# Attention issued at a planner offset of 700 in a two-layer hybrid attention backbone

## Chip, cores and metric

One core of a Trainium2 chip runs the whole program. The metric is device time in microseconds (us) of one execution. The engines are TensorE (PE; its weight loads are listed apart as PEld), VectorE (DVE), ScalarE (ACT), GpSimd (POOL) and SyncE (SP). Each works through its own list of instructions in the order fixed when the program is built. An instruction that waits holds up all that stand behind it on its engine. SP issues most DMAs, ACT some.

## What is computed

Two layers over 512 latent tokens and 256 context tokens of width 1024, in float32. Each layer has one mixer with three head groups of eight heads and a gate:

```
def layer(x, cx, ...):
    hx = rmsnorm(x, norm_w) * (1 + scale) + shift          # the context likewise: hc
    px, pc = split_cols(hx @ w_in), split_cols(hc @ w_in)  # q, k, v of A, B, C, and the gate
    ya, yca = global_gqa(...)            # A: all latent and all context keys; RMS-normed q/k, rotary
    yb, ycb = neighbourhood_attn(...)    # B: a window of 8 x 16 on the grid, learned bias, plus context
    yc_, ycc = window_gqa(...)           # C: +-128 tokens, a sink logit per head, plus context
    ux = concatenate([ya, yb, yc_]) * silu(px[9])
    x = x + gate * (ux @ w_out)          # the context likewise, except in the last layer
```

The result is the latent stream after a final RMS norm.

## The kernel before

**Numbers.** Every float32 operand of a product is split into a rounded high part (fp32r) and a low remainder, and a product is three matmuls (high x high, high x low, low x high). For weights, `split` (L244) copies a staged tile `ws` to `wh` on ACT (L247) and subtracts on DVE or POOL to get `wl` (L250). Three staging buffers and five pairs of split buffers run ahead of the matmuls.

**Projections.** `proj_f` (matmuls at L318, up to 512 columns) and `proj_t` (L341, 256 columns, two token tiles to a bank) multiply the normed stream `hL`, `hC` by the weights into a PSUM bank `pj`, of which there are two. When a bank is complete, a function `done` handles the result: for A's q and k it copies the bank to `qs` (L821), squares, applies norm and rotary (L830 to L840, on POOL for most q), splits into `qd`, transposes `qd` on PE into a bank T (L899) and copies T to `qt` on ACT (L902). For C it copies to `tA` (L973); after it, DMAs swap halves into `tB`, POOL multiplies and adds (L979 to L981), and Q and K are split on ACT and POOL (L989, L990). For gates it takes a tanh `th` (L879) and a multiply (L880).

**Attention.** A pair of heads is one entry of work, with one unit per head (two per head for A) and, in the first layer, one more per head for the context queries. A unit's `scores` multiply Q by K into the PSUM tensor `Sbig` (matmuls at L1049), take the negated maximum `negm` on DVE (L1158, L1121, or with a mask or bias added L1208 and L1265) and the exponential `P` on ACT (L1160, L1127, L1211, L1267). Its `values` transpose P into a bank T (L1054; two banks, shared with `done`), copy it to `pth` on ACT (L798), subtract on DVE to `ptl` (L1044), and multiply both by V into `Obig` (L1049). `finish` (L1315) divides by the sums, applies the gate and stores the pair's result `u`. B's bias is built inside `scores` when first needed: two loads on SP, a row `wr` (L1437) and a mask `bm` (L1440), and three additions on POOL (L1445). In `attend` (L1375) a unit's values run with the next unit's scores, so a pair's last values and its `finish` fall into the next stage.

**Stages.** The list `PLAN` (L33) sets the order: first projections alone; then, stage by stage, the attention of one pair is woven with the projections that later pairs need: B0 to B3, then A0, C0, A1, C1, A2, C2, A3. Last comes C3, woven with the first columns of the output projection (`head`, matmuls at L519). So the q of A1 is projected while C0 attends, and the q of C1 while A1 attends.

**Order.** `weave` (L1407) takes steps of attention and of projection in turn, in proportion to estimates in the planner's own units (`TA`, L1503, and `time`, L1520; they follow the columns streamed at full rate): in the second layer 16.5 for an A pair, 12.5 for a B or C pair, 10.6 for one pair's q and gate. It also ties every third projection matmul behind an attention matmul that stands `lead` = 6 of these units earlier in the same stage (`paced`, L296), so that projections do not run further ahead than that.

The framework's planner turns this into the lists. Each instruction takes the next number of a counter. The planner simulates the engines, and an engine that is free takes, among the instructions whose inputs and buffers are ready, the one with the lowest number. A block under `high_priority(offset=n)` numbers its instructions from n below the counter, and hands the counter back as it was. All `done` calls stand in such blocks, with offset 600 (`hp`, `hpf`). Weight loads and splits, the projections' matmuls and the attention take the counter as it is. Only the last attention (`rest`, C3) stands in blocks already, of offset 0 (`hr`).

Of the kernel before, what the change touches and what calls it, by code (L numbers as in the profile page):

```python
# [19 lines left out]
D = 1024  # L20
# [26 lines left out]
AT_ONCE = (2, 3)  # L47
RSPAN = 7 * 31 + 48

CFG = dict(lead=6.0, hp=600, hpf=600, pj=2, T=2, O=1, P=5, qt=5, kt=4, vt=4, gt=3, wh=5, ws=3, pt=3, bm=2, tA=1, OT=1, u=1, tl=1, ab="pj", tR=1, map={}, ada=2, h0=300, h1=1000, a0=9, H=2, hr=0, cp="A", cv="A", w0="D", w1="D", w2=(("D", "D"), ("D", "D")), hb="D", ws_="P")  # L50

WT_A_KV, WT_A, WT_BV, WT_BG = 0, 1, 5, 7
WF_BQ, WF_BK, WF_CQ, WF_CK, WF_CV, WF_CG = 0, 4, 8, 12, 13, 14
# [10 lines left out]
def body(tc, xT, small, bcast, rpb, adaw, adat, wt, wf, wo, trigA, trigC, mskB, mskC, outT):  # L64
    nc = tc.nc
    es = ExitStack()
    const = es.enter_context(tc.tile_pool(name="const", bufs=1))
    wpool = es.enter_context(tc.tile_pool(name="w", bufs=CFG["wh"]))
    hpool = es.enter_context(tc.tile_pool(name="h", bufs=16))
# [21 lines left out]
    def pj():  # L91
        return ps.tile([128, 512], F32, name="pj", bufs=CFG["pj"])

    Sbig = ps.tile([128, 1536], F32)

    def psT():
        return ps.tile([128, 512], F32, name="T", bufs=CFG["T"])

# [57 lines left out]
    class Dots:  # L156


        def __init__(self):
            self.jobs = [(h, j) for h in range(2) for j in range(KT)]  # L160
            self.n = self.at = self.wait = 0
            self.room = [qkv.tile([128, 3, 512], F32, name="dots", tag="vt", bufs=CFG["vt"]) for _ in range(2)]
            self.rows(0)
# [77 lines left out]
    pace = {"at": None, "pe": None, "dve": None, "sp": None}  # L241
    wlo = {"n": 0, "by": CFG["w0"]}

# [10 lines left out]
    def load_w1(dram_ap, i, shape):  # L254
        st = wpool.tile([128, 512], F32, name="ws", bufs=CFG["ws"])
        pace["sp"] = nc.sync.dma_start(st, dram_ap[:, i * 512:(i + 1) * 512]).ins.name
        return split(st, shape)
# [284 lines left out]
    for l in range(2):  # L542
        last = l == 1
        with tc.tile_pool(name=f"p1_{l}", bufs=1, reuse_waits="tile") as p1:
            mixers(tc, nc, l, last, p1, ps, const, dict(locals()))
# [226 lines left out]
def mixers(tc, nc, l, last, p1, ps, const, env):  # L772
    g_ = env
# [179 lines left out]
    def tables_c():  # L953
        for c in range(2):
            t = p1.tile([128, NT], F32, name=f"tabx{c}", tag=f"tab{c}", bufs=1)
            nc.sync.dma_start(t, trigC[c])
            tabs["C", c] = t
# [330 lines left out]
    def units(kind, i, Q, K, V, G, extra):  # L1288
        c = dict(kind=kind, i=i, Q=Q, G=G)
        out = []  # L1290
        for h in range(2):
            if kind == "B":
                vh, k, sink = h, K[h], None
                box = []

                def bm(h=h, box=box):
                    if not box:
                        box.append(extra(2 * i + h))
                    return box[0]
            else:  # L1300
                vh = i // 2
                k = K[vh]
                j = l * 8 + 2 * i + h
                sink = negsink[:, j:j + 1] if kind == "C" else None
                bm = (lambda: extra)
            v = lambda kb, vh=vh: V[:, kb, vh].rearrange("p x f -> p (x f)")
            if kind == "A":
                out += [GlobalUnit(c, h, k, v, tiles=t) for t in ((0, 1), (2, 3))]
            else:
                out.append((NearUnit if kind == "B" else BandUnit)(c, h, k, v, sink, bm))  # L1310
            if not last:
                out.append(CtxUnit(c, h, k, v, sink))
        return c, out
# [57 lines left out]
    def chain(gens):  # L1371
        for g in gens:
            yield from g

    def attend(pair):  # L1375

        if pair is not None:
            c, us = pair
            for n, un in enumerate(us):
                sc = un.scores()  # L1380
                yield from zipped(chain(pend), sc)
                pend.clear()
                pend.append(un.values())
            pend.append(finish(c, c["kind"] == "C" and c["i"] == 3))

    def zipped(a, b):

        ta = tb = 0.0
        a, b = iter(a), iter(b)
        la = lb = True  # L1390
        while la or lb:
            if la and (ta <= tb or not lb):
                try:
                    x = next(a)
                    ta += x
                    yield x
                except StopIteration:
                    la = False
            else:
                try:  # L1400
                    x = next(b)
                    tb += x
                    yield x
                except StopIteration:
                    lb = False

    def weave(a, ta, b, tb, lead=CFG["lead"]):  # L1407

        xa = xb = 0.0
        la = a is not None  # L1410
        past = []
        pace["pe"] = None
        while True:
            if la and xa * tb <= xb * ta:
                try:
                    xa += next(a)
                    past.append((xa, pace["pe"]))
                except StopIteration:
                    la = False
            else:  # L1420
                while len(past) > 1 and past[1][0] <= xa - lead:
                    past.pop(0)
                pace["at"] = past[0][1] if past and past[0][0] <= xa - lead else None
                try:
                    xb += next(b)
                except StopIteration as r:
                    pace["at"] = None
                    if la:
                        for _ in a:
                            pass  # L1430
                    return r.value
# [24 lines left out]
    def bias_c():  # L1456
        m = p1.tile([128, 896], F32, name="msk", tag="bm", bufs=CFG["bm"])
        nc.sync.dma_start(m, mskC)

        def bm(i):  # L1460
            return m[:, (384, 256, 0, 0)[i]:(896, 896, 640, 512)[i]]
        return bm
# [5 lines left out]
    def ada_pre():  # L1468
        if ada_jobs:
            job = ada_jobs.pop(0)  # L1470
            ada_next.append((job, ada_load(job, g_["qkv"], "vt", CFG["vt"])))
# [13 lines left out]
    def with_ada(gen, t, k):  # L1485

        n, x, nxt = 0, 0.0, t / 2 / max(k, 1)
        while True:
            try:
                y = next(gen)  # L1490
            except StopIteration as r:
                while n < k:
                    one_piece()
                    n += 1
                return r.value
            x += y
            if x > nxt and n < k:
                one_piece()
                n += 1
                nxt += t / k  # L1500
            yield y

    TA = {"A": 16.5, "B": 12.5, "C": 12.5, None: 1.0}  # L1503
    TC = 0.0 if last else 2.7
    tq = 5.3 if last else 7.8
    prev = None
# [17 lines left out]
    def work(items, bank):  # L1524
        for k, i in items:
            made[k, i] = yield from make[k](i, bank)
# [4 lines left out]
    for pair, items, n_ada in PLAN:  # L1531
        if pair is None and not last:

            items = items[1:] + items[:1]
        if pair is not None:
            kind, i = pair
            if kind == "B":
                Q, K = made["b", i]
                prev = units("B", i, Q, K, made["v", i // 2][i % 2], lambda i=i: made["g", i // 2][i % 2], bmb)
            else:  # L1540
                Q, G = made[kind.lower(), i]
                K, V = made[kind.lower() + "kv", 0]
                prev = units(kind, i, Q, K, V, G, bmc if kind == "C" else None)
        if pair == ("A", 0):
            tables_c()
            bmc = bias_c()
            if not last:
                ada_pre()
        wlo["by"] = CFG["w1"] if pair is None or pair[0] == "B" else CFG["ws_"]
        t = sum(time[k] for k, i in items)  # L1550
        gen = with_ada(work(items, first if pair is None else pj), t, n_ada[last])

        soon = 1.5 if last and pair == ("A", 3) else 1.0
        weave(attend(prev) if prev else None, TA[kind] + TC if prev else 1.0, gen, t * soon)
    Q, G = made["c", 3]
    K, V = made["ckv", 0]
    prev = units("C", 3, Q, K, V, G, bmc)

    def rest():
        yield from attend(prev)  # L1560
        yield from chain(pend)

    def urgent(gen):
        while True:
            with tc.high_priority(offset=CFG["hr"]):
                try:
                    x = next(gen)
                except StopIteration:
                    return
            yield x  # L1570

    weave(urgent(rest()), TA["C"] + TC, g_["head"](l, p1), CFG["H"] * (7.5 if last else 8.0), 3.0)


def col_index():
# [95 lines left out]
```

## Time and profile before

| what | value |
|---|---|
| time, median of 3 runs | 1198.84 us (1198.54 to 1199.2) |
| span of the profiled execution, from its first to its last instruction (the profile gives no other time of it) | 1197.7 us |
| PE busy | 1150.5 us, 8016 matmuls |
| DVE, ACT, POOL busy | 769.4, 696.9, 408.1 us |
| mean granted PE clock | 0.996 of full |
| scores of B, first and second layer (from L1265) | 86 to 257 us, 738 to 886 us |
| scores of A, first and last in a layer (L1158) | 268 to 550 us, 888 to 1103 us |
| scores of C, first and last in a layer (L1208) | 325 to 580 us, 930 to 1129 us |
| bytes moved by DMA | 124.22 MB |

"Busy" of PE counts each matmul from its start to its modelled end, which overlaps the next one, so a PE that is busy all the time need not be at its peak. An idle stretch of PE is one in which no matmul was under way at all. Below, lines of a list read: start, duration, engine, line of the kernel, operation, result <- operands, shape, count, and in brackets the engine's idle time just before and what ended it. A line with "<-" and a colon reads: who waited, for whom, in total us, how often, the longest.

### The profile page before, as it was taken

The numbers are of one execution on the slowest core, as the hardware profiler recorded it, in microseconds if no ns is written. First come the engines' busy times: TensorE is split into PE (matmuls) and PEld (weight loads), VectorE is DVE, ScalarE is ACT, GpSimd is POOL, SyncE is SP. The second block draws the span as 40 slices with busy tenths as digits, with TensorE's granted clock in tenths as the row PEclk, the third lists the DMA queues.
The fourth block names the chain that finished last, engine by engine and source line by source line (L and its number), as shares of the span: only waits on it lengthen the run. The fifth ranks groups of instructions, "written<-read, shape, count | busy, mean of one in ns | idle before, by whom it ended". The sixth has DMA issues, their size and how long they took to land.

```text
span 1197.7 us, 21749 instructions
## 1 busy us (share of the span) xinstructions
PE 1150.5 (96%) x8016; PEld 1034.8 (86%) x8016; DVE 769.4 (64%) x1548; ACT 696.9 (58%) x1581; POOL 408.1 (34%) x496
## 2 busy tenths in 40 slices
PE   5999999999999999999999999999999999998997
PEld 3898999998898988988778999989988888887876
DVE  5767566764656665568578895567754556567563
ACT  5446555656666676588423544555666667677552
POOL 1341110234446354385000030202274563656001
PEclk9999999999999999999999999999999999999999
DMA  9552222313312112123086662323222111232152
GB/s 321 213 142 89 78 78 67 123 66 104 111 70 92 67 44 92 34 63 119 27 293 198 205 210 74 98 84 109 91 73 67 53 46 53 63 88 72 36 161 77
DMA packets 60826, 124.22 MB, mean 104 GB/s; under 512 B 7216, under 2 KB 13488, under 8 KB 60720
## 3 DMA queue, kind: packets, MB, share of 16 engines
q1 hardware_dynamic: 54768, 111.96, 29.6%
q10 hardware_dynamic: 5952, 10.88, 2.7%
q8 instruction: 63, 1.03, 0.3%
q14 instruction: 43, 0.35, 0.1%
HBM read 109.05 MB, written 11.14 MB: 100 GB/s over the span
## 4 chain that ended last, share of the span: by engine, by line
PE 81%; DVE 5%; ACT 5%; DMA 3%; issue 3%; POOL 1%; SPq 0%; ACTq 0%; DVEq 0%; POOLq 0%
PE pj L318 18%; PE pj L341 17%; PE Sbig L1049 9%; PE Obig L1049 9%; PE T L1054 9%; PE pj L519 5%; PE T L519 3%; PE Sbig L519 3%; PE T L341 2%; PE Sbig L430 2%; DVE ptl L1044 1%; DMA x<-xT_dram 1%; PE Sbig L341 1%; ACT pth L798 1%; PE pj L430 1%
## 5 line engine op out<-in xcount | busy, mean ns | idle before, releaser
L1044 DVE TENSOR_TENSOR ptl<-T,pth 128x512 fp32r<-128x512 f32 (+2 forms) x312 | 181.1, 591 | 128.6 <-ACT pth L798 126.7
L798 ACT ACTIVATE pth<-T 128x512 fp32r<-128x512 f32 (+2 forms) x312 | 158.9, 520 | 134.8 <-PE T L1054 128.1
L341 PE MATMUL pj<-wh,hL 128*128 128x256 f32 x896 | 180.6, 287 | 0.0
L318 PE MATMUL pj<-hL,wh 128*128 128x512 f32 x544 | 175.0, 401 | 0.9 <-ACT wh L247 0.5
L1054 PE MATMUL T<-ident,P 128*128 128x128 f32 x1024 | 165.7, 273 | 4.0 <-ACT qt L902 1.7
L247 ACT ACTIVATE wh<-ws 128x512 fp32r<-128x512 f32 x192 | 119.5, 629 | 78.6 <-PE pj L318 16.3
L1049 PE MATMUL Sbig<-kt,qt 128*128 128x256 f32 (+1 forms) x864 | 156.2, 308 | 4.6 <-ACT P L1160 2.5
L250 POOL TENSOR_TENSOR wl<-ws,wh 128x512 fp32r<-128x512 f32 x76 | 98.5, 1300 | 146.4 <-ACT wh L247 146.4
L341 PEld LDWEIGHTS pj<-wh,hL 128*128 128x128 f32 x896 | 144.2, 190 | 1.0 <-issue 0.2
L1049 PE MATMUL Obig<-pth,vt 128*128 128x256 f32 (+2 forms) x432 | 134.6, 321 | 4.6 <-ACT pth L798 2.0
L1054 PEld LDWEIGHTS T<-ident,P 128*128 128x128 f32 x1024 | 123.0, 140 | 17.6 <-DVE ptl L1044 2.2
L1049 PE MATMUL Obig<-ptl,vt 128*128 128x256 f32 (+2 forms) x432 | 131.4, 318 | 5.0 <-DVE ptl L1044 4.3
L1049 PEld LDWEIGHTS Sbig<-kt,qt 128*128 128x128 f32 x864 | 123.3, 189 | 13.4 <-DVE negm L1208 4.1
L341 PE MATMUL pj<-wl,hL 128*128 128x256 f32 x448 | 128.0, 286 | 0.0
L318 PEld LDWEIGHTS pj<-hL,wh 128*128 128x128 f32 x544 | 96.2, 189 | 16.7 <-ACT wh L247 0.9
L250 DVE TENSOR_TENSOR wl<-ws,wh 128x512 fp32r<-128x512 f32 x116 | 82.7, 720 | 40.4 <-ACT wh L247 31.6
L318 PE MATMUL pj<-hL,wl 128*128 128x512 f32 x272 | 107.1, 394 | 0.5 <-DVE wl L250 0.5
L1049 PEld LDWEIGHTS Obig<-pth,vt 128*128 128x128 f32 x432 | 81.6, 189 | 15.9 <-ACT pth L798 7.1
L1049 PEld LDWEIGHTS Obig<-ptl,vt 128*128 128x128 f32 x432 | 81.5, 189 | 14.7 <-DVE ptl L1044 11.3
L1445 POOL TENSOR_TENSOR bm<-wr,bm 128x192 f32<-128x192 f32 (+1 forms) x48 | 41.3, 888 | 139.6 <-DMA bm<-mskB_dram 132.4
L341 PEld LDWEIGHTS pj<-wl,hL 128*128 128x128 f32 x448 | 85.4, 191 | 0.3
L1158 DVE TENSOR_REDUCE negm<-Sbig 128x1 f32<-128x768 f32 x64 | 61.0, 953 | 29.7 <-PE Sbig L1049 15.7
(336 smaller groups left out, 2495.6 us busy)
## 6 DMA issues: line engine op xcount, KB each, us to landing
ws<-wf_dram SPq DMA_DIRECT2D x72, 256.0 KB, 3.1
ws<-wt_dram SPq DMA_DIRECT2D x72, 256.0 KB, 3.0
ada<-adaw_dram SPq DMA_DIRECT2D x32, 512.0 KB, 5.5
ws<-wo_dram SPq DMA_DIRECT2D x57, 256.0 KB, 2.8
bm<-mskB_dram SPq DMA_DIRECT2D x16, 576.0 KB, 3.7
dw<-adat_dram SPq DMA_DIRECT2D x8, 512.0 KB, 8.2
dots<-adat_dram SPq DMA_DIRECT2D x16, 256.0 KB, 4.5
u<-u ACTq DMA_DIRECT2D x9, 384.0 KB, 2.9
```

What stands on the lines that cost most here:

```text
L247: nc.scalar.activation(hi, src, AF.Copy)
L250: eng.tensor_sub(lo, src, hi.bitcast(F32))
L318: paced(nc.tensor.matmul(p[:, 0:n], a[:, r, :], cols(b[kt], c0, n), start=(i == 0), stop=(i == 23)), i)
L341: paced(nc.tensor.matmul(p[:, t * 256:(t + 1) * 256], tok(a[kt], t2 + t), b[:, r, :], start=(i == 0), stop=(i == 23)), i)
L430: mm = nc.tensor.matmul(out, a, b, start=begin, stop=(kt == KT - 1 and i == 2), skip_group_check=True)
L519: mm = nc.tensor.matmul(p[:, 0:n], a[:, r, :], ucols(ua[b][ft], c0, n), start=(ft == FT_ORDER[0] and i == 0), stop=(ft == FT_ORDER[-1] and ...
L798: nc.scalar.activation(out, src, AF.Copy)
L1044: i = nc.vector.tensor_sub(lo[:, 0:n], T[:, 0:n], hi[:, 0:n].bitcast(F32))
L1049: m = nc.tensor.matmul(*args, **kw)
L1054: m = nc.tensor.transpose(*args, **kw)
L1158: nc.vector.tensor_reduce(nm, S, axis=AX.X, op=OP.max, negate=True)
L1445: nc.gpsimd.tensor_add(b, src, b)
```

## The change

The wrapper `urgent` moves up and takes its offset as an argument, a new setting `ha` = 700 joins the configuration, and in every stage the attention of the pair is run through the wrapper. Each step that the weave takes from the attention is then one block of offset 700. The block holds all that the step issues: matmuls, transposes, copies, the exponentials, POOL's additions and products, B's two loads on SP and the stores of `u`. The last attention keeps offset 0. Nothing else is touched.

```diff
-CFG = dict(lead=6.0, hp=600, hpf=600, ..., h0=300, h1=1000, a0=9, H=2, hr=0, ...)
+CFG = dict(lead=6.0, hp=600, hpf=600, ..., h0=300, h1=1000, ha=700, a0=9, H=2, hr=0, ...)
...
+    def urgent(gen, offset):
+        while True:
+            with tc.high_priority(offset=offset):
+                try:
+                    x = next(gen)
+                except StopIteration:
+                    return
+            yield x
...
-        weave(attend(prev) if prev else None, TA[kind] + TC if prev else 1.0, gen, t * soon)
+        weave(urgent(attend(prev), CFG["ha"]) if prev else None, TA[kind] + TC if prev else 1.0, gen, t * soon)
...
-    def urgent(gen):
-        while True:
-            with tc.high_priority(offset=CFG["hr"]):
-                try:
-                    x = next(gen)
-                except StopIteration:
-                    return
-            yield x
-
-    weave(urgent(rest()), TA["C"] + TC, g_["head"](l, p1), CFG["H"] * (7.5 if last else 8.0), 3.0)
+    weave(urgent(rest(), CFG["hr"]), TA["C"] + TC, g_["head"](l, p1), CFG["H"] * (7.5 if last else 8.0), 3.0)
```

More of the change, by code (lines that the diff above doesn't have):

```diff
@@ L48 @@
 RSPAN = 7 * 31 + 48
-CFG = dict(lead=6.0, hp=600, hpf=600, pj=2, T=2, O=1, P=5, qt=5, kt=4, vt=4, gt=3, wh=5, ws=3, pt=3, bm=2, tA=1, OT=1, u=1, tl=1, ab="pj", tR=1, map={}, ada=2, h0=300, h1=1000, a0=9, H=2, hr=0, cp="A", cv="A", w0="D", w1="D", w2=(("D", "D"), ("D", "D")), hb="D", ws_="P")
+CFG = dict(lead=6.0, hp=600, hpf=600, pj=2, T=2, O=1, P=5, qt=5, kt=4, vt=4, gt=3, wh=5, ws=3, pt=3, bm=2, tA=1, OT=1, u=1, tl=1, ab="pj", tR=1, map={}, ada=2, h0=300, h1=1000, ha=700, a0=9, H=2, hr=0, cp="A", cv="A", w0="D", w1="D", w2=(("D", "D"), ("D", "D")), hb="D", ws_="P")
 WT_A_KV, WT_A, WT_BV, WT_BG = 0, 1, 5, 7
```

## Prediction

> **What bounds the kernel now.** I read the page's first lines, then busy time by stretch, then what TensorE (PE) waited for, then two pieces of the timeline. Columns of the stretch view: length, then busy time of PE, of its weight loads (PEld), of VectorE (DVE), ScalarE (ACT) and GpSimd (POOL), each with its instruction count, then clock, DMA share and GB/s.
>
> ```profile
> span 1197.7 us, 21749 instructions
> PE 1150.5 (96%) x8016; PEld 1034.8 (86%) x8016; DVE 769.4 (64%) x1548; ACT 696.9 (58%) x1581; POOL 408.1 (34%) x496
> ```
> ```profile
> 86.00:262.00 176.00, 175.44 (x1321) 166.47 (x1321) 118.02 (x263) 102.63 (x255) 31.01 (x57) 1.00 0.27 85
> 738.00:886.00 148.00, 147.51 (x1084) 138.32 (x1082) 98.34 (x219) 83.06 (x199) 36.95 (x56) 1.00 0.31 92
> 262.00:600.00 338.00, 330.09 (x2369) 295.04 (x2368) 211.17 (x415) 220.33 (x513) 165.34 (x189) 1.00 0.24 75
> 886.00:1090.00 204.00, 196.94 (x1301) 174.72 (x1302) 117.41 (x218) 139.81 (x306) 114.96 (x130) 1.00 0.22 66
> 1090.00:1144.00 54.00, 49.68 (x299) 42.06 (x298) 36.86 (x68) 32.97 (x70) 10.09 (x10) 1.00 0.11 33
> ```
>
> PE is the bound: it idles 1197.7 - 1150.5 = 47.2 us. The B stages (the first two rows, cut at the times of B's scores) leave 0.6 and 0.5 us of that, the A and C stages (the next two) 7.9 and 7.1, the last unit 4.3: 19.3 us is what a better order could remove outside B. No matmul goes, so the rest of the 1198 us stays.
>
> Inside the A and C stages the idle time is bunched. The next rows are eight stretches that I chose by the largest PE waits (two of the rows, and their sum); the last row is the projections' line L318 alone in 1090 to 1106.
>
> ```profile
> 944.00:958.00 14.00, 12.05 (x81) 10.12 (x80) 8.17 (x20) 9.76 (x25) 9.47 (x11) 1.00 0.28 94
> ...
> 1090.00:1106.00 16.00, 12.49 (x87) 10.62 (x86) 14.18 (x22) 13.60 (x27) 9.03 (x8) 1.00 0.09 28
> sum 134.00, PE 121.62 PEld 103.63 DVE 89.65 ACT 101.21 POOL 80.38; mean PE 15.20 PEld 12.95 DVE 11.21 ACT 12.65 POOL 10.05
> ```
> ```profile
> 1090.00:1106.00 16.00, 0.00 (x0) 0.00 (x0) 1.00 0.09 28
> ```
>
> The eight hold 134.0 - 121.6 = 12.4 us of idle PE. There PE has little but attention to do, and attention waits for its own chain: transposes into T, ACT copies pth, DVE subtracts ptl, PE multiplies into Obig. PE's waits, in total, times and longest:
>
> ```profile
> PE Obig L1049 <- DVE ptl L1044: 4.3, 11, 0.8
> PE Obig L1049 <- ACT pth L798: 2.0, 6, 0.5
> PE T L1054 <- DVE ptl L1044: 1.8, 3, 0.9
> PE T L1054 <- ACT qt L902: 1.7, 2, 1.2
> ```
>
> One of them in the timeline, at the start of an A stage:
>
> ```profile
> 948.73 0.36 ACT L821 ACTIVATE qs<-pj 128x256 f32<-128x256 f32 x1
> 948.74 0.60 PE L1054 MATMUL T<-ident,P 128*128 128x128 f32 x4
> 949.00 0.37 ACT L879 ACTIVATE th<-pj 128x256 f32<-128x256 f32 x1
> 949.26 0.63 ACT L247 ACTIVATE wh<-ws 128x512 fp32r<-128x512 f32 x1
> 949.78 0.65 ACT L902 ACTIVATE qt<-T 128x256 fp32r<-128x256 f32 x2
> 950.31 0.61 ACT L798 ACTIVATE pth<-T 128x512 fp32r<-128x512 f32 x1
> 950.49 0.44 PE L1054 MATMUL T<-ident,P 128*128 128x128 f32 x2 [1.15 <-ACT qt L902]
> ```
>
> The attention's transposes of 948.74 ended at 949.34, but ACT first did qs and th, a weight split, and qt; pth began 0.97 us later, and the next transposes waited 1.15 us for qt to empty their T bank. Three of those four ACT operations handle projection results, which today have an offset of 600; the split has none.
>
> **The change part by part.** Nothing is added or removed: every matmul, copy and DMA stays. Each attention instruction gets a planner number 700 lower, and as its block hands the counter back, attention no longer advances it. Its number now lies below every projection's of its stage and the one before, and below that of a result handled (offset 600) less than 100 numbers earlier. I price six consequences.
>
> 1. *Result handling steps behind attention.* Worth at most the four waits above, 4.3 + 2.0 + 1.8 + 1.7 = 9.8 us; at least 0, since many of those waits are the chain itself. The two waits for qt (1.7 us) go, and some behind pth and ptl: **-3 us** (0 to -9.8).
>
> 2. *Projections remain where attention waits.* Attention goes first whenever it is ready, so projections serve as filler instead of running ahead. The eight stretches idle 12.4 us; less the 3 of step 1, 9.4 are left. What was late behind the stalls is next: A's first scores need Q, and its softmax must run before the first transposes; no order fills that while a projection may lead attention by only 6 planner units. I take half, **-5 us** (0 to -9.4).
>
> [...]
>
> 3. *The cushion in the B stages goes.* There attention is not pressed today. Two ptl and the multiplies that use them:
>
> ```profile
> 139.87 0.68 DVE L1044 TENSOR_TENSOR ptl<-T,pth 128x512 fp32r<-128x512 f32 x1
> ...
> 141.16 0.69 DVE L1044 TENSOR_TENSOR ptl<-T,pth 128x512 fp32r<-128x512 f32 x1
> ...
> 144.66 0.39 PE L1049 MATMUL Obig<-ptl,vt 128*128 128x512 f32 x1
> ...
> 145.59 0.41 PE L1049 MATMUL Obig<-ptl,vt 128*128 128x512 f32 x1
> ```
>
> The operands lay ready 4.1 and 3.7 us, so no jitter of ACT or DVE reaches PE. Issued as soon as the plan thinks them ready, they lose this, and every difference between plan and chip stalls an in-order PE. Bounds: 0, and the A and C stages' rate: 15.0 us in 542 is 2.8%, on 324 us of B stages 9 us. As plenty of projections lie between, I stay near the lower end: **+2 us** (0 to +9).
>
> 4. *Results come later.* Behind attention, the handling and the weight splits wait on ACT and DVE, and POOL's splits and rope behind its mask adds and u's. What PE feels is the next stage's Q. In the example qs began at 948.73 and Q's transposes at 959.15:
>
> ```profile
> 959.15 0.45 PE L899 MATMUL T<-identr,qd 128*128 128x128 f32 x4
> ```
> ```profile
> L902 ACT ACTIVATE qt<-T 128x256 fp32r<-128x256 f32 x40 | 13.1, 380 | 7.8 <-PE T L899 6.9 <-ACT tA L973 0.7
> L341 PE MATMUL pj<-wh,hL 128*128 128x256 f32 x896 | 180.6, 287 | 0.0
> ```
> ```profile
> 79.88 5.76 PE pj L341 x48
> ```
>
> With two copies of qt that is 10.4 + 0.45 + 0.76 = 11.6 us. The first unit needs only the first of two or three token pairs; a pair is 48 matmuls, 5.8 us in the last row (from the chain). The lead lets 6 of an A stage's 16.5 planner units (TA, L1503) pass, and with them 6 x 10.6 / 16.5 = 3.9 units of projections (time, L1520), by the planner's scale some 4 us. That covers 9.8 of 11.6 us, and attention's own work the rest. I take **0 us**; if 1.5 us are left bare at each of the 14 changes into an A or C stage, +21.
>
> 5. *DMAs and queues.* With attention move 16 mask loads and 16 bias rows on SP, the stores of u on ACT's queue, POOL's mask adds, and the 1/sum products.
>
> ```profile
> bm<-mskB_dram SPq DMA_DIRECT2D x16, 576.0 KB, 3.7
> ```
> ```profile
> SPq L1440 <- DVE negm L1265: 68.0, 11, 15.0
> ```
>
> The load waits for its buffer, not for its turn, and three staging buffers of weights stand behind it: **0 us**; if one in four of the 16 held up weights for its 3.7 us, +15.
>
> 6. *Attention's own order.* Neighbouring blocks now share numbers, so a step's transposes can mix with the next's. Four take 0.33 us of PE; a chain may end that much later, and as many earlier, while other attention and projections fill PE: **0 us** (-3 to +3).
>
> Sum: -3 - 5 + 2 = -6 us. The profiled execution spans 1197.7, 1.1 us under the median 1198.84; that edge is outside every step, so 1197.7 - 6 + 1.1 = **1192.8 us**.
>
> **The rivals.**
>
> *Everything is reclaimed.* Steps 1 and 2 reach their limits together, the 19.3 us of idle PE outside B, and B stays full: 1198.8 - 19 = 1180 us. For it: stretches with no projection at all. Against: the softmax at a stage's start stays. [...]
>
> *Nothing changes.* Where attention is behind, its numbers are already the lowest ready ones, and where it is ahead PE is full either way (175.44 of 176.00). Then 1198.8 +- 2.4. If the order is hardly moved, the change doesn't do what it says, with the same time.
>
> *Slower: Q, K and rope come late.* Place: the change into each A or C stage. Attention has used up its tail of values, which fills PE today between 948 and 958, before the projections of its stage end; then the 11.6 us chain stands with only the 4 us of lead and its own last projections over it. It decides once what is left bare at a change exceeds 0.4 us, since 14 x 0.4 takes back the 6 us won. Price: 14 x 1.5 = 21, less 6: 1198.8 + 15 = 1214 us. For it: ACT is busy 70% and POOL 68% from 944 to 958, so the handling would queue. Against: the first token pair's early start.
>
> More idle PE can also cost clock: in 600 to 650 the granted clock fell to 0.97, after two waits of 1.40 and 1.37 us within 3 us.
>
> ```profile
> 600.00:650.00 50.00, 47.21 (x231) 39.01 (x230) 41.07 (x68) 15.13 (x27) 0.00 (x0) 0.97 0.76 261
> ```
> ```profile
> 623.01 0.73 PE L519 MATMUL pj<-hL,wh 128*128 128x512 f32 x2 [1.40 <-ACT wh L247]
> 625.12 0.77 PE L519 MATMUL pj<-hL,wl 128*128 128x512 f32 x1 [1.37 <-DVE wl L250]
> ```
>
> The first row is 0.03 x 50 = 1.5 us lost; five such drops make the rival 1221. [...]
>
> **How the numbers follow.** Forecast (1186 to 1196.4): 0.36. All reclaimed (below 1186): 0.13. Nothing (within 0.2%, 2.4 us, about what a measurement of this kernel can tell from no change): 0.17. Slower: 0.34. So faster 0.49, same 0.17, slower 0.34. Predicted 1192.8. The range runs from 1178 (nearly all of the 19.3 us gone) to 1215 (the slower rival); 0.10 lies above it, 0.05 below. The faster cases' own range is 1178 to 1196.
>
> **What would show it.** Step 1: no wait of T for qt, and pth right behind its transposes. Step 2: projections of L318 or L341 in stretches like 944 to 958, and less idle PE in the A and C stages than 15.0 us. Step 3: ptl to multiply well under 4 us in the B stages, with their idle PE at 1 to 3 us. Step 4: scores waiting for qt or kt at stage changes would prove it wrong. Step 5: a wait of wh for ws. The forecast is wrong if B stages lose more than the A and C stages win, or if PE stands waiting for results at stage changes.

## The result, and the profile after

The changed kernel takes 1206.65 us (1203.09 to 1209.15, 6 runs) against 1199.02 us (1198.07 to 1200.48, 6 runs): ratio 1.0055, 95% interval 1.0040 to 1.0071. It is slower by some 7 us (7.6 between the medians, 6.6 by the ratio); the forecast had it 6 us faster. It lies inside the range of 1178 to 1215, about midway between the rivals "nothing changes" (1198.8) and "slower" (1214), and not near the forecast.

The first lines of the page of the changed kernel:

```profile
span 1205.0 us, 21737 instructions
...
PE 1154.6 (96%) x8016; PEld 1036.6 (86%) x8016; DVE 771.3 (64%) x1548; ACT 695.4 (58%) x1581; POOL 406.1 (34%) x496
```

Idle PE rose from 47.2 to 50.4 us. Busy PE rose by 4.1 us with the same 8016 matmuls: some 1.7 us of it go with a drop of the clock at A1's start, shown further below, and the rest is not traced. Of the 7.3 us between the two spans (1197.7 and 1205.0) most are lost early: the first score of A in the first layer starts at 268.1 us (268.5 before), the first of B in the second layer at 743.8 (738.0), the first of A there at 894.4 (887.9). Busy time by stretch, same columns as before; the stretches follow the same stages, cut 4 us later at the end of the first layer's and 7 to 8 us later in the second:

```profile
86.00:262.00 176.00, 175.97 (x1332) 167.51 (x1331) 118.85 (x262) 103.28 (x256) 31.56 (x58) 1.00 0.28 86
262.00:604.00 342.00, 331.83 (x2360) 294.93 (x2359) 209.01 (x413) 219.25 (x511) 163.39 (x188) 1.00 0.23 74
746.00:893.00 147.00, 145.81 (x1076) 136.75 (x1075) 99.15 (x218) 81.92 (x198) 39.17 (x58) 1.00 0.29 91
893.00:1097.00 204.00, 196.82 (x1305) 174.75 (x1303) 119.54 (x217) 140.01 (x305) 113.65 (x128) 1.00 0.22 66
```

The first layer's A and C stages idle 10.2 us in 342 (7.9 in 338 before), the second's 7.2 in 204 (7.1). B's first layer is fuller than before (0.03 us idle against 0.56), its second layer emptier (1.19 in 147 against 0.49 in 148). PE's largest waits inside the layers, in total, times, longest:

```profile
PE Obig L1049 <- DVE ptl L1044: 4.7, 12, 0.7
PE Obig L1049 <- ACT pth L798: 2.7, 7, 0.6
...
PE T L1054 <- DVE ptl L1044: 2.1, 4, 0.9
...
PE T L1054 <- ACT qt L902: 1.9, 3, 1.2
PE T L899 <- POOL qd L895: 1.8, 3, 0.9
```

None of the four waits of step 1 went; each is 0.2 to 0.7 us longer. The prediction's own example, at 950.49, is still there, 5.9 us later and just as long, with the same ACT operations in the same order ahead of `pth`:

```profile
956.39 0.44 PE L1054 MATMUL T<-ident,P 128*128 128x128 f32 x2 [1.15 <-ACT qt L902]
```

The last row of the list is new and leads to the cause: the transposes of Q wait for POOL's `qd`.

**A3's start in the first layer.** Lines of the timeline of the kernel before, from the last q of A3 (copied to `qs`) to its transposes:

```profile
514.78 0.38 ACT L821 ACTIVATE qs<-pj 128x256 f32<-128x256 f32 x1
...
515.31 0.74 POOL L830 TENSOR_TENSOR tC<-qs,tab 128x256 f32<-128x256 f32 x1
...
517.96 2.21 POOL L1340 TENSOR_TENSOR tR<-onesw,rec 128x128 f32<-128x128 f32 x6
...
522.33 0.61 POOL L840 TENSOR_TENSOR tC<-tC,ssA 128x256 f32<-128x256 f32 x1
...
523.38 0.42 ACT L894 ACTIVATE qd<-tC 128x256 fp32r<-128x256 f32 x1
...
524.90 0.45 PE L899 MATMUL T<-identr,qd 128*128 128x128 f32 x4
```

The same in the changed kernel:

```profile
516.00 0.38 ACT L821 ACTIVATE qs<-pj 128x256 f32<-128x256 f32 x1
...
517.43 0.75 POOL L830 TENSOR_TENSOR tC<-qs,tab 128x256 f32<-128x256 f32 x1
...
521.16 2.21 POOL L1340 TENSOR_TENSOR tR<-onesw,rec 128x128 f32<-128x128 f32 x6
...
524.42 0.61 POOL L840 TENSOR_TENSOR tC<-tC,ssA 128x256 f32<-128x256 f32 x1
...
525.03 0.90 ACT L1160 ACTIVATE P<-Sbig,negm 128x768 f32<-128x768 f32 x1
...
526.27 0.42 ACT L894 ACTIVATE qd<-tC 128x256 fp32r<-128x256 f32 x1
...
528.06 0.54 PE L899 MATMUL T<-identr,qd 128*128 128x128 f32 x4
```

From `qs` to the transposes it was 10.1 us and is now 12.1. The 2 us come at three places. POOL begins with `qs` (L830) 1.43 us after it instead of 0.53, since a weight split's subtraction ahead of it ends later. When L840 ends, at 525.03, ACT takes attention's exponential and comes to `qd` 1.24 us later, where it was 0.44 us. And POOL's part of `qd` (L895) starts 1.0 us after ACT's instead of 0.5, behind a product of C's rotary step (L980). POOL's 1/sum products (L1340, attention's) stand in this chain in both kernels. Meanwhile PE has no projection. In the stretch view, all of PE and then line L318 alone, before:

```profile
518.80:525.50 6.70, 6.00 (x37) 4.69 (x36) 4.52 (x8) 4.79 (x12) 4.63 (x9) 1.00 0.33 80
518.80:525.50 6.70, 0.00 (x0) 0.00 (x0) 1.00 0.33 80
```

and in the changed kernel:

```profile
519.30:528.90 9.60, 7.44 (x37) 4.92 (x38) 6.14 (x11) 6.65 (x16) 7.47 (x13) 1.00 0.24 68
519.30:528.90 9.60, 0.00 (x0) 0.00 (x0) 1.00 0.24 68
```

In each stretch PE runs 37 matmuls and no projection. It lasts 9.6 us instead of 6.7, and its idle time grows from 0.7 to 2.2 us.

**A3's start in the second layer** shows who goes first on ACT. Before, and then changed:

```profile
1072.34 0.42 ACT L894 ACTIVATE qd<-tC 128x256 fp32r<-128x256 f32 x1 [1.01 <-POOL tC L840]
1072.66 0.71 ACT L1211 ACTIVATE P<-P,negm 128x512 f32<-128x512 f32 x1
...
1072.83 0.74 POOL L895 TENSOR_TENSOR qd<-tC,qd 128x256 fp32r<-128x256 f32 x1 [0.53 <-ACT qd L894]
...
1074.25 1.29 POOL L980 TENSOR_TENSOR tB<-tB,tabx 128x512 f32<-128x512 f32 x1 [0.69 <-DMA tB<-tA]
...
1075.26 0.46 PE L899 MATMUL T<-identr,qd 128*128 128x128 f32 x4
```
```profile
1077.75 0.72 ACT L1211 ACTIVATE P<-P,negm 128x512 f32<-128x512 f32 x1 [0.77 <-DVE negm L1208]
...
1078.47 0.40 ACT L894 ACTIVATE qd<-tC 128x256 fp32r<-128x256 f32 x1
...
1079.92 1.29 POOL L980 TENSOR_TENSOR tB<-tB,tabx 128x512 f32<-128x512 f32 x1 [1.96 <-DMA tB<-tA]
...
1081.18 0.72 POOL L895 TENSOR_TENSOR qd<-tC,qd 128x256 fp32r<-128x256 f32 x1
...
1081.95 0.28 PE L899 MATMUL T<-identr,qd 128*128 128x128 f32 x1 [0.65 <-POOL qd L895]
```

Attention's exponential now stands ahead of `qd` on ACT. On POOL the order has turned too: C's rotary product L980, which has a higher number than either, now comes ahead of the subtraction L895 that ends `qd`, and stands 1.96 us for its own DMA, so that L895 starts 2.7 us after ACT's part instead of 0.5. PE waits 0.65 us for the result.

### The profile page after: what moved, and what is told of

The parts are those of the page before. It is cut to its first block, busy times and chain, and to the rows that moved or that the text cites. A ratio compares the mean times of both kernels' runs of the same rounds, so it can differ in the third digit from the quotient of the medians.

```text
span 1205.0 us, 21737 instructions
## 1 busy us (share of the span) xinstructions
PE 1154.6 (96%) x8016; PEld 1036.6 (86%) x8016; DVE 771.3 (64%) x1548; ACT 695.4 (58%) x1581; POOL 406.1 (34%) x496
## 5 line engine op out<-in xcount | busy, mean ns | idle before, releaser
L318 PE MATMUL pj<-hL,wh 128*128 128x512 f32 x544 | 176.3, 402 | 0.5 <-ACT wh L247 0.5
L1054 PE MATMUL T<-ident,P 128*128 128x128 f32 x1024 | 172.7, 273 | 3.8 <-ACT qt L902 1.7
L247 ACT ACTIVATE wh<-ws 128x512 fp32r<-128x512 f32 x192 | 119.5, 629 | 75.3 <-PE pj L318 16.5
L1049 PE MATMUL Obig<-ptl,vt 128*128 128x256 f32 (+2 forms) x432 | 134.7, 324 | 5.4 <-DVE ptl L1044 4.7
L318 PEld LDWEIGHTS pj<-hL,wh 128*128 128x128 f32 x544 | 96.0, 189 | 15.9 <-ACT wh L247 0.9
L318 PE MATMUL pj<-hL,wl 128*128 128x512 f32 x272 | 107.3, 394 | 0.0
L1158 DVE TENSOR_REDUCE negm<-Sbig 128x1 f32<-128x768 f32 x64 | 61.1, 955 | 31.2 <-PE Sbig L1049 17.1
```

Source lines behind the costliest of these rows:

```text
L247: nc.scalar.activation(hi, src, AF.Copy)
L318: paced(nc.tensor.matmul(p[:, 0:n], a[:, r, :], cols(b[kt], c0, n), start=(i == 0), stop=(i == 23)), i)
L1049: m = nc.tensor.matmul(*args, **kw)
L1054: m = nc.tensor.transpose(*args, **kw)
L1158: nc.vector.tensor_reduce(nm, S, axis=AX.X, op=OP.max, negate=True)
```

## The experiments

Every ratio is to runs of the kernel before in the same job; its 95% interval, in brackets, is 0.1% to 0.2% to each side. The expectations use letters. R: results are handled late, behind attention. N: the renumbering (blocks that hand the counter back) costs. L: the kernel before is one favourable order, and any other order differs by luck. M and P are told where they come in.

**Which part of the change (lead 6.0).** Offset 0 for all attention leaves the renumbering alone; the next two give 700 to some stages and 0 to the rest; the fourth keeps 700 and lets the counter run on over attention.

```diff
-ha=700                                          # e1_offset0
+ha=0
-urgent(attend(prev), CFG["ha"])                 # e3_only_B; e4_only_AC has != "B"
+urgent(attend(prev), CFG["ha"] if kind == "B" else 0)
+                n = tc.cur_priority             # e5_no_renumber, inside the block, ahead of next(gen)
...
+                n = tc.cur_priority - n
+            tc.cur_priority += n if offset else 0
```

> The wrapper stays round the attention of every stage, but with offset 0: attention keeps the counter's numbers and only stops advancing it. Theory R (results late: result handling and rope, put behind attention, come late from POOL and block ACT's queue): the loss is gone, 1199 +- 2 us, and ACT's waits for POOL between 262 and 600 us are back near 4.9 us from 13.3. Rival N (renumbering: neighbouring attention blocks share numbers and mix): the loss stays, 1206 +- 2. Rival L (luck of the order: any reshuffle of a finely fitted order costs some us): anything from 1197 to 1210, with no relation to what moved.

Measured: 1205.75 us, ratio 1.0042 (1.0027 to 1.0056).

> Offset 700 in the B stages alone, offset 0 in the A and C stages. Theory R: B's results need no rope on POOL, so nothing is lost there: 1199 +- 2 us. Rival N: as much as offset 0 everywhere. My prediction's step 3 (cushion of the B stages) would give 1201 to 1208.

Measured: 1201.48 us, 1.0003 (0.9991 to 1.0014).

> Offset 700 in the A and C stages alone, offset 0 in the B stages. Theory R: the whole loss, 1206 +- 2 us, with ACT's waits for POOL between 262 and 600 us near 13. Rival L: B-only and AC-only do not add up to the change's 7.6 us.

Measured: 1213.15 us, 1.0106 (1.0089 to 1.0123).

> Attention at offset 700 as in the changed kernel, but the counter advances over attention as before, so no two steps of attention share numbers. N (the renumbering costs, the offset itself does little): the renumbering alone lost 0.42%; without it the time is within 0.2% of the kernel before, some 1200 us. Added up from the earlier runs (renumbering +5, offset in B -4.5, offset in A and C +7.5) it would be +2 to +3 us. L (any order that differs loses or wins a few us at a few places where engines meet badly): between -0.3% and +0.6%, with the losses at single places and one of them near 280 to 296, where C's keys are split.

Measured: 1209.29 us, 1.0067 (1.0046 to 1.0088).

R missed two of its figures: e1 was to be back at 1199 us, and e4 near 1206. The renumbering isn't what the changed kernel loses by: without it the time is no better. By the sums, 700 in the A and C stages costs 0.64% (e4 against e1) or 0.52% (changed against e3), and 700 in B gives 0.39% or 0.51% back. At this point L wasn't excluded.

**Results ahead of attention.** The changed kernel with the handling of results at 1400.

```diff
-hp=600, hpf=600
+hp=1400, hpf=1400
```

> Attention at 700 as in the change, and the handling of results at 1400 instead of 600, so above attention again; only projections, weight loads and splits and the rope after the handling are below attention. Theory R: most of the loss is gone, 1199 to 1202 us. Rival N: 1206 +- 2. Rival L: anything from 1197 to 1210.

Measured: 1208.94 us, 1.0066 (1.0051 to 1.0081). R seemed to fall. The trace has the stretch without projections at A3's start in the first layer back at its old length, but the one at A2's start grew from 6.8 to 10.1 us, and near 289 us PE stalls for 2.84 us.

**The stall near 285 us.** Where A0's attention meets the splitting of C's keys, the changed kernel lost 1.3 us and e1 3.2 us of PE in 12. First before, then changed, then e1:

```profile
284.00:296.00 12.00, 12.00 (x80) 10.79 (x80) 7.00 (x14) 7.21 (x16) 5.63 (x4) 1.00 0.28 93
```
```profile
284.00:296.00 12.00, 10.66 (x70) 9.50 (x70) 8.39 (x11) 8.39 (x20) 5.36 (x4) 1.00 0.24 69
```
```profile
284.00:296.00 12.00, 8.80 (x48) 8.11 (x47) 8.43 (x10) 6.42 (x15) 4.62 (x3) 0.72 0.07 22
```

There VectorE's cast L1001 takes 0.95 us where it starts just ahead of POOL's second subtraction L1000 (which then takes 2.62 us, the first 1.83), and 1.69 us (changed) or 2.49 us (e1) where it started second. Before, changed, and e1:

```profile
282.64 4.52 POOL L1000 TENSOR_TENSOR kt<-tR,kt 64x768 fp32r<-64x768 f32 x2 [1.24 <-ACT kt L999]
...
284.50 0.95 DVE L1001 CAST kt<-kt 64x1536 fp32r<-64x1536 f32 x1 [0.39 <-POOL kt L1000]
```
```profile
282.90 3.75 POOL L1000 TENSOR_TENSOR kt<-tR,kt 64x768 fp32r<-64x768 f32 x2 [0.96 <-ACT kt L999]
...
285.78 1.69 DVE L1001 CAST kt<-kt 64x1536 fp32r<-64x1536 f32 x1
```
```profile
285.16 2.49 DVE L1001 CAST kt<-kt 64x1536 fp32r<-64x1536 f32 x1
```

So M: the cast blocks attention's VectorE work behind it. The test moves L1000 to VectorE, in the changed kernel and in the one before.

```diff
-cklo="P"
+cklo="D"
```

> The changed kernel with one setting more: the low part of C's keys (L1000) is subtracted on VectorE and not on POOL, so the cast of L1001 on VectorE no longer runs beside a POOL subtraction of the same tile. M (the cast and POOL's tensor operation exclude each other; the one that starts second waits, and when it is VectorE the attention behind it is late): the two subtractions cost VectorE some 1.9 us, the cast is back to 0.95 us in every instance, PE idles under 0.7 us in 284 to 296 instead of 1.34, and the kernel is 1 to 3 us faster than the changed one, that is 1203.5 to 1205.5 in the terms of its 1206.65 us. L: the gap moves elsewhere, the time is within 1 us of the changed kernel's or anywhere from 1200 to 1210.

Measured: 1215.17 us, 1.0109 (1.0090 to 1.0128).

> The kernel before with the same setting. M: nothing to win where POOL and not VectorE waited; PE had no idle time at all in 284 to 296; within 0.1% of the kernel before, and if it falls with the last run by the same amount, the cast isn't what tells the two orders apart. L: -0.2% to +0.5%, since the order changes from 280 us on.

Measured: 1207.77 us, 1.0047 (1.0029 to 1.0064).

M's small steps came: both casts of e6 take 0.95 us and PE idles 0.31 us in 284 to 296. The gain didn't: from 278 to 296 PE was busy 16.66 us in the changed kernel and 16.80 in e6, and both kernels are some 0.5% slower with the edit. M falls as a lever. That the kernel before, whose priorities are untouched, loses 0.47% by an edit of two small operations speaks for L.

**Neighbours of both kernels.** Only `lead` is changed, in the kernel before and in the changed one. P: the attention's priority itself costs, whatever the order around it.

```diff
-lead=6.0
+lead=6.2                                        # e8, e11; 5.8 in e9, e10 and 6.1 in e12, e13
```

> A control: the kernel before with lead 6.2 instead of 6.0. No priority changes; attention stands 3% further ahead of the projections tied to it. N and M: nothing touched, within 0.2% of the kernel before. L: a few us away, like the changed kernel, with the difference at a few places; the sign is open (0.997 to 1.006).

Measured: 1211.93 us, 1.0075 (1.0057 to 1.0094).

> The kernel before with lead 5.8. Lead 6.2 cost 0.75%. If the kernel before is one favourable order among its neighbours (L), lead 5.8 is slower as well, +0.2% to +1%. If lead 6.2 was slow because a longer lead is worse, lead 5.8 is within 0.2% or faster.

Measured: 1218.3 us, 1.0148 (1.0131 to 1.0164).

> The kernel before with lead 6.1, the smallest step of the three. L: +0.1% to +1%, even this step leaves the favourable order, with losses of 1 to 3 us near 280 to 296 and 705 to 715. If the time follows the lead smoothly: between 1.000 and 1.0075, near 1.004. P says nothing of it.

Measured: 1210.41 us, 1.0074 (1.0056 to 1.0093).

> The changed kernel with lead 6.2, to be set against the kernel before with lead 6.2 (ratio 1.0075). P: 1.0075 + 0.0055 = 1.013 of the kernel before. L: anywhere from 1.000 to 1.013, as soon under 1.0075 as over it.

Measured: 1218.88 us, 1.0153 (1.0137 to 1.0169).

> The changed kernel with lead 5.8, to be set against the kernel before with the same lead. P (the attention's priority itself costs some 6 us): slower than that one by 0.4% to 0.7%, as at lead 6.0. L (the priority costs nothing by itself; the kernel before at 6.0 is a favourable order, and every change of the order leaves it): either sign, between -0.6% and +0.6%, and the mean of the pairs at 5.8 and 6.2 is near nothing.

Measured: 1223.81 us, 1.0197 (1.0181 to 1.0212).

> The changed kernel with lead 6.1, to be set against the kernel before with lead 6.1 (1.0074). P (the priority itself costs): 0.4% to 0.8% slower than that one, 1.0115 to 1.0155 of the kernel before. L (it costs nothing by itself): as soon under 1.0074 as over it.

Measured: 1209.66 us, 1.0082 (1.0068 to 1.0096).

Both are partly right. The kernel before at 6.0 is a favourable order: every neighbour with untouched priorities, even 0.1 of lead away, is 0.47% to 1.48% slower. Yet the changed kernel is also slower than its own partner (differences of ratios): by 0.49%, 0.55% and 0.78% at leads 5.8, 6.0 and 6.2 and 0.62% with the moved subtraction, but by 0.08%, inside the intervals, at 6.1. Luck alone would hardly give four of five pairs nearly the same loss.

**The same parts at lead 6.2.** The edits of the first group, at the other lead.

```diff
-lead=6.0, ha=700                                # e14; e15 and e16 keep ha and have the weave's line above
+lead=6.2, ha=0
```

> Lead 6.2, all attention in blocks of offset 0: the renumbering alone. If the renumbering carries the cost: 1.0117 or more (1.0075 and the 0.42% of lead 6.0). If the offset carries it: near 1.0075, and under the changed kernel's 1.0153 of that lead.

Measured: 1210.64 us, 1.0087 (1.0073 to 1.0100).

> Lead 6.2, offset 700 in the B stages, 0 in A and C. If A and C carry the cost: near the kernel before with lead 6.2 (1.0075), as it was near the kernel before at lead 6.0. L: anywhere from 1.000 to 1.015.

Measured: 1209.93 us, 1.0077 (1.0064 to 1.0089).

> Lead 6.2, offset 700 in the A and C stages, 0 in B. If A and C carry the cost: at or over the changed kernel's 1.0153. L: anywhere from 1.000 to 1.018.

Measured: 1217.36 us, 1.0134 (1.0121 to 1.0148).

| attention at 700 | lead 6.0 | lead 6.2 |
|---|---|---|
| nowhere (kernel before) | 1 | 1.0075 |
| nowhere, renumbered | 1.0042 | 1.0087 |
| in B | 1.0003 | 1.0077 |
| in A and C | 1.0106 | 1.0134 |
| in all (changed) | 1.0055 | 1.0153 |

The offset in A and C costs 0.64%, 0.52%, 0.47% and 0.76% in the four pairs of rows that differ by it alone; B's offset -0.39%, -0.51%, -0.10% and +0.19%. The cost comes from the offset in the A and C stages.

**The handling put back ahead of attention.** Two causes fit: attention ranks over the projections' matmuls, or over the handling of their results. Results at 1400 undo the second alone. e17 is e4 with that edit, e18 is e11.

```diff
-hp=600, hpf=600                                 # e17 beside the weave's line of e4, e18 beside lead=6.2
+hp=1400, hpf=1400
```

> Lead 6.0, offset 700 in the A and C stages alone, and the handling of results at 1400, so that it stays ahead of attention. The run without the last edit took 1.0106, the one with offset 0 everywhere 1.0042. R (the cost in A and C is that the last q of an A pair is handled behind attention): the last q's copy qs to its transposes is back at 9.8 to 11.4 us where it was 12.2 and 12.4, the stretches without a projection matmul near 461 and 1082 are gone, and the time is near 1.0042 (1.003 to 1.006). If the cost is attention ahead of the projections' matmuls: it stays at 1.009 to 1.012.

Measured: 1204.11 us, 1.0023 (1.0012 to 1.0034).

> Lead 6.2, the changed kernel with the handling of results at 1400. The changed kernel took 1.0153 at this lead, offset 0 everywhere 1.0087. R: back to 1.007 to 1.011. If attention ahead of the projections' matmuls costs: 1.013 to 1.017.

Measured: 1212.01 us, 1.0092 (1.0075 to 1.0109).

Both fall back: 1.0106 to 1.0023 (offset 0: 1.0042), 1.0153 to 1.0092 (offset 0: 1.0087). So the cost in A and C goes when the handling of results is put ahead again, and attention's rank over the projections' matmuls alone costs nothing that shows. One run stands against it: e2, the same edit on the changed kernel at lead 6.0, wins nothing (1.0066 against 1.0055). Its stall of 2.84 us can't be why, for e17 has one of 2.71 us at the same place. The timeline of e17 at A3's start in the second layer has `qd` ahead of the exponential again:

```profile
1076.47 0.42 ACT L894 ACTIVATE qd<-tC 128x256 fp32r<-128x256 f32 x1 [1.01 <-POOL tC L840]
1076.79 0.71 ACT L1211 ACTIVATE P<-P,negm 128x512 f32<-128x512 f32 x1
...
1079.35 0.45 PE L899 MATMUL T<-identr,qd 128*128 128x128 f32 x4
```

At A3's start in the first layer the time from `qs` to the transposes is 9.8 us.

The next table sets all kernels side by side at the starts of A1, A2 and A3 in both layers. *Handlings*: the six times from the pair's last `qs` (L821) to the first of its transposes (L899), added up. *Turned*: at how many of the six POOL takes C's product L980 ahead of `qd`'s L895. *PE idle*: PE's idle time in the six stretches from that `qs` to 4 us past that first transpose. For the kernel before and the changed one it comes from these sums of the six:

```profile
sum 83.89, PE 76.80 PEld 62.50 DVE 57.33 ACT 65.72 POOL 60.04; mean PE 12.80 PEld 10.42 DVE 9.55 ACT 10.95 POOL 10.01
```
```profile
sum 85.92, PE 75.12 PEld 59.54 DVE 54.26 ACT 63.47 POOL 58.92; mean PE 12.52 PEld 9.92 DVE 9.04 ACT 10.58 POOL 9.82
```

| kernel | handlings, us | turned | PE idle, us | ratio |
|---|---|---|---|---|
| before | 59.9 | 0 | 7.1 | 1 |
| e1, e3, e17 | 59.9, 60.9, 60.9 | 0, 0, 0 | 6.8, 6.5, 6.9 | 1.0042, 1.0003, 1.0023 |
| changed, e4 | 61.9, 64.8 | 3, 2 | 10.8, 10.8 | 1.0055, 1.0106 |
| e2, e5 | 61.1, 63.0 | 1, 2 | 10.3, 10.9 | 1.0066, 1.0067 |
| e7, e6 | 57.7, 63.3 | 0, 3 | 6.0, 11.2 | 1.0047, 1.0109 |
| lead 6.2: e8, e15, e18 | 59.6, 60.7, 61.6 | 0, 1, 1 | 12.4, 11.6, 11.8 | 1.0075, 1.0077, 1.0092 |
| lead 6.2: e14, e16, e11 | 63.4, 65.2, 66.1 | 1, 3, 3 | 11.3, 13.4, 13.0 | 1.0087, 1.0134, 1.0153 |
| lead 6.1: e12, e13 | 61.8, 61.7 | 2, 1 | 10.6, 10.6 | 1.0074, 1.0082 |
| lead 5.8: e9, e10 | 70.6, 70.5 | 3, 3 | 10.3, 10.2 | 1.0148, 1.0197 |

These measures were chosen after seeing the traces, one profiled execution of each kernel, so they support the runs and don't replace them. At lead 6.0 they part the kernels cleanly: PE idles 6.0 to 7.1 us at the starts in the kernel before, in those without the offset in A and C (e1, e3, e7) and in e17, and 10.3 to 11.2 us in all others. That answers e2: its edit put results first by number, but the plan that came out is still late at A1 and A2 (2.0 and 2.9 us idle, 0.7 and 0.9 before). Why the same rank gives a good order in e17 and a bad one in e2 stays open; so does the reason why the two, which differ only by B's offset, are 0.43% apart when that offset won 0.4% to 0.5% in the other pairs at this lead. The idle time also fits the odd pair: at 6.1 both kernels idle equally there, and they are equally fast. And it tells part of what makes the order of the kernel before favourable: its neighbours by lead idle 3 to 5 us more at these starts.

Two things it doesn't tell. At 5.8 the two kernels idle equally and are 0.49% apart. And the idle time at the starts, some 4 us more at lead 6.0 and 1 to 2 at 6.2, is less than half of the 10 and 7 us that e17 and e18 win back; the rest isn't traced to the handling (the mean granted clock of the profiled executions was 0.993 in e4 and 0.994 in e17, 0.992 in e11 and 0.994 in e18).

Most of what e17 still loses to the kernel before lies near 285 us: one wait of PE there is 2.71 us long, for VectorE's `OT`, and the clock falls (compare the same stretch above):

```profile
284.00:296.00 12.00, 9.29 (x57) 8.49 (x55) 8.53 (x10) 7.70 (x18) 6.12 (x4) 0.86 0.16 55
```

No run beat the kernel before.

## Why the prediction was wrong, step by step

*What bounds the kernel* held: PE is busy to 96% in both, and idle PE (3.7 us) and clock (1.7 us) at the starts of A's stages are a good part of the difference.

*Steps 1 and 4* failed, and they are one step seen from two sides: step 1 booked -3 us for putting the handling of results behind attention, step 4 booked 0 (up to +21) for their coming late. The runs show no gain and the whole cost: 0.47% to 0.76% of 1200 us, 5.6 to 9.1 us, for the offset in A and C, and it goes when the handling is put ahead again in e17 and e18 (not in e2).

Step 1's error was to take a rank for an order. The waits of T for `qt`, which were to vanish, went from 1.7 to 1.9 us, and the quoted example came back unchanged. Of the four ACT operations ahead of its `pth` three had begun (948.73, 949.00 and 949.26) before the transposes ended at 949.34: a lower number can't put an operation first that isn't ready. Why the fourth, `qt`, kept its place is not shown.

Step 4's error was its cover of 0 us: attention's own work was to hide what the lead does not. At A3's start that work is there, and PE idles 2.2 us in 9.6, 1.4 of them in waits for `ptl` and 0.5 in one for `pth`, since that work is a chain that waits for itself. What step 4 put at nothing measured 3.7 us of idle PE at the six starts (7.1 to 10.8) and 1.7 us of clock at one of them. Nor did it see that a late `qd` loses its place on POOL to C's rotary product.

*Step 2* (-5 us) didn't come. Idle time of A and C rose by 2.4 us, and in e17, where attention ranks over the projections but not over results, nothing clear of the noise was won either (1.0023 against 1.0042 with offset 0, with intervals that overlap). That the lead and not the rank holds the projections back is my reading; the two weren't tried apart.

*Step 3* (+2) was wrong in kind: at the place that it quoted, the cushion of the B stages is still there.

```profile
139.15 0.68 DVE L1044 TENSOR_TENSOR ptl<-T,pth 128x512 fp32r<-128x512 f32 x1
...
140.15 0.69 DVE L1044 TENSOR_TENSOR ptl<-T,pth 128x512 fp32r<-128x512 f32 x1 [0.32 <-ACT pth L798]
...
143.92 0.39 PE L1049 MATMUL Obig<-ptl,vt 128*128 128x512 f32 x1
...
144.72 0.40 PE L1049 MATMUL Obig<-ptl,vt 128*128 128x512 f32 x1
```

The operands lie ready 4.1 and 3.9 us (4.1 and 3.7 before). B's idle time hardly moved, from 1.05 to 1.22 us, and the offset in B made the kernel faster at lead 6.0 (by 0.39% and 0.51%), not slower, and did little at 6.2 (-0.10% and +0.19%); why is not shown.

*Step 5* held: ACT's waits of `wh` for a weight tile `ws`, which were its sign, fell from 16.5 to 13.6 us.

*Step 6* (0, ±3) was too small: the renumbering alone costs 0.42% at lead 6.0, 5 us, which the stall near 285 us and its clock (3.2 us idle, 0.28 x 12 = 3.4 us of clock) cover, and 0.12% at 6.2.

*The rivals.* The slower one named the mechanism, Q late at stage starts behind attention. Its price was too high and its place too wide: not 1.5 us at each of 14 changes, but 3.7 us of idle PE at the six that were measured, the starts of A1 to A3 in both layers (by start: from 0.7, 0.9, 0.9, 2.0, 1.6 and 0.9 us to 1.0, 1.6, 2.6, 2.5, 1.6 and 1.4). The changes into A0 and the C stages were not measured apart. Its clock drop was seen too:

```profile
369.80:373.30 3.50, 3.45 (x17) 3.39 (x18) 1.03 (x3) 2.41 (x6) 0.56 (x1) 0.51 0.00 0
```

Half the clock for 3.5 us at A1's start in the first layer costs 0.49 x 3.5 = 1.7 us. The kernel before didn't pay it there.

*What was missing among the rivals* is that the kernel before sits at a favourable point, so that an edit which only reorders starts with a debt: 0.47% to 1.48% in the four neighbours with untouched priorities. How often an untried edit would be luckier, no run shows.

## What to carry to other kernels

Before raising one class of work above another, list what the lower class hands to the next stage: here a 10 us chain over three engines feeds Q, and up to 2 us of delay on it at a few places cost more than the 3 us of waits that were to go. Then look whether the engines' lists have changed where you meant them to: a rank acts only among operations that are ready, and one that comes late can lose its place to work that ranks lower. Test a scheduling edit as a pair, with and without it, at two or three settings of an unrelated knob; a single comparison against a tuned order mixes the edit's cost with the loss of that order's luck. If attention is to rank higher, rank the handling of results higher still, and look at the order that comes out: it helped in e17 and e18, not in e2.

## What the runs showed of the hardware

Where the VectorE cast of 64x1536 (L1001) met a POOL subtraction of 64x768 (L1000), the one that started second took longer. In the kernel before that was POOL's second subtraction: 2.62 us against 1.83 for the first, 4.52 us for the two, where the changed kernel has 3.75. In the changed kernel and in e1 it was the cast: 1.69 and 2.49 us instead of 0.95, and it ended 0.82 and 0.81 us after the subtraction. That looks as if the second waits for the first; by what means, no trace shows.

In the changed kernel the granted clock fell to 0.51 for 3.5 us at A1's start, though PE was busy for most of the time ahead of it. The 3.4 us ahead of the drop:

```profile
366.40:369.80 3.40, 2.41 (x11) 1.42 (x10) 2.41 (x5) 3.02 (x8) 1.96 (x3) 1.00 0.21 48
```

PE was busy for 71% of them (2.41 / 3.40), its weight loads for 42%, and no wait of PE in them was longer than 0.33 us. Near 285 us the clock was 0.86 over 284 to 296 in e17, with a wait of PE of 2.71 us in it, and 1.00 in e2, with one of 2.84 us. What the clock follows, no run shows.
